# First mixer of a fused network on one core: attention and scan heads taken two at a time

## The chip, the cores and the metric

One core of a Trainium2 chip runs the whole network in one launch. The metric is device time in microseconds (us), from the runs of the program on that core: smaller is better. TensorE (PE in the views) multiplies, VectorE (DVE) and ScalarE (ACT) do the elementwise work, and one queue of transfers (SP) moves data between HBM and the on-chip memory. The products of TensorE land in PSUM, which has eight banks.

## The reference

Two blocks of layers stand behind one another, on 256 tokens of 1024 features, in float32. The first layer's mixer is what the change touches. It projects the normed input and has two branches of 16 heads with 64 features each:

```python
def na_branch(qkv, rpb):           # attention in a window of a 2-D grid
    ...
        s = jnp.einsum('bwhd,biwjhd->bhwij', q_r, k_win) + bias.transpose(0, 2, 1, 3)[None]
        p = jax.nn.softmax(s.reshape(Bsz, NA_HEADS, GRID_W, kh * NA_KW), axis=-1).reshape(s.shape)
        return jnp.einsum('bhwij,biwjhd->bwhd', p, v_win)

def ssd_scan(xh, dt, a, bm, cm):   # state space scan, run in both directions
    ...
    cb = jnp.einsum('bctgn,bcsgn->bgcts', Cc, Bc)
    y_diag = jnp.einsum('bgrcts,bcsgrp->bctgrp', cb[:, :, None] * Lmat, X)
```

The two results are normed, joined and multiplied with an output matrix. The kernel computes the scan of a head as one 256 by 256 matrix of decays (both directions added) times `cb`, applied to the head's 64 columns of tokens; and the attention of a head as full 256 by 256 scores with a bias that is -1e30 outside of the window.

## The kernel before, in words

Weights come in units of 1 MB ([128, 2048] float32). Each unit is split on chip into a high and a low part (`wh` by ACT on line 350, `wl` by DVE on line 359, two halves each), and each large product is three TensorE products of high and low parts. These are the rows `mm<-...` in the views.

`mixer0` (line 960) walks 21 such units in the order of `M0_ORDER` (line 28): four units for the scan's input (`in_x`, line 1105), four gates (`in_z`), and four times q, k, v for four attention heads each (`in_na`, line 1127). Between units, `tick` runs steps of small chains, which are Python generators: `ssd_heads` (line 1026) and `na_heads` (line 1075), one head per step, four heads per chain, so sixteen heads in each branch.

A step of attention (`step` on line 1082) loads the head's bias (`nb`, 256 KB, line 1085, two buffers), multiplies q and k into a PSUM tile `sp` (line 1088, on 64 rows of the array: the head's 64 features lie in partitions 0 to 63 or 64 to 127), adds the bias and takes the row maxima on DVE (line 1091), runs exponentials, division and four transposes of the result (`softmax_T`, line 913; ACT line 350, PE line 369), copies the transposed table to `smp`, and multiplies it with v into half of the partitions of `yp` (line 1096, on 64 columns of the array).

A step of the scan (line 1030) loads the cumulative decays as a broadcast (`bp`, line 1033, two buffers), builds the exponentials (`decay`, line 945), multiplies them with `cb` into `qt`, and multiplies `qt` with the tokens `xt` into half of the partitions of its `yp` (line 1043, on 64 columns).

These small products are in float32, not split: one instruction of the program shows as two rows in the trace, so that a head of each of the three kinds (scores `ax<-nk,nq`, values `ax<-smp,nv`, scan `ax<-qt,xt`) has two instructions and four rows.

The order of the instructions on each engine is fixed when the program is built, by a scheduler that may move instructions past one another where their data permit; `issue_after` and `order` (line 884) bind it. On the chip each engine takes its instructions in that order. Four PSUM banks (`mm`) are for large products, four (`ax`) for everything else. `conv_tile` (line 933) uses padded buffers `cvp` (line 993), three in rotation.

Of the kernel before, what the change touches and what calls it, by code (L numbers as in the profile page):

```python
# [26 lines left out]
# order of the steps of the first mixer (x, z, q/k/v of attention; b: further background) and of the third one  # L27
# [3 lines left out]
# heads of the memory's keys and values that are projected at the ends of the layers' parts  # L31
FILLERS = [("k0 k1", "mm"), ("v0 v1", "ax"), ("k2 k3", "mm"), ("v2 v3", "ax")]
# units of the gated feed-forward that are computed by tokens first, and how many of them wait for their transposes
# [12 lines left out]
# ---------------------------------------------------------------- layout of the inputs  # L46
# [33 lines left out]
# the projections of the third mixer: name, first column, number of columns  # L80
# [11 lines left out]
def _units(w):  # L92
    """[1024, 256 m] -> m units [128, 8 * 256]"""
    m = w.shape[1] // T
    return w.reshape(8, P, m, T).transpose(2, 1, 0, 3).reshape(m, P, 2048)


def _down(w):
    """[256 m, 1024] -> m units [128, 2 * 1024]"""
    m = w.shape[0] // T  # L100
    return w.reshape(m, 2, P, D).transpose(0, 2, 1, 3).reshape(m, P, 2048)


def _square(w):
    """[512, 512 m] -> m units [128, 4 * 512]"""
    m = w.shape[1] // 512
    return w.reshape(4, P, m, 512).transpose(2, 1, 0, 3).reshape(m, P, 2048)
# [13 lines left out]
def prepare(i):  # L121
# [114 lines left out]
    # neighbourhood bias: entry (row distance, column distance), NEG outside of the window  # L236
# [29 lines left out]
# ---------------------------------------------------------------- the program  # L266

class Stack:
# [31 lines left out]
    # ---- small helpers  # L300
# [5 lines left out]
    def phase(self, name, mm=4, apart=(), swap=False):  # L306
        """tiles that live within one phase of the program; mm of the eight banks are for the large products;
        apart: tags with pools of their own, so that they lie where the neighbouring phases leave room in time"""
# [65 lines left out]
    # ---- steps of a chain that are put between the units of the large products  # L374
# [3 lines left out]
    def tick(self, n=1, background=1):  # L378
        """n steps of the chains in order (a chain that yields True waits for others), some of the background's
        (fractions add up)"""  # L380
# [21 lines left out]
    @contextmanager  # L402
    def held(self, on=True):
        """what is traced here is issued after the norm that ended the last phase"""
        with ExitStack() as st:
            for ins in self.hold if on else ():
                st.enter_context(self.tc.issue_after(ins.ins))
            yield

    def lagged(self, steps):  # L410
        """generator: each step's second part after the next one's first part"""
# [17 lines left out]
    # ---- weights: a unit is [128, 2048], taken as high and low parts in two halves  # L429
# [24 lines left out]
    def small_unit(self, name):  # L454
        """generator: a few columns for all inputs, in pieces of 512 of a tile's columns"""
# [11 lines left out]
    def proj_tok(self, u, xh, xl, kind="mm", after=False):  # L467
        """256 columns of x @ W -> [128 tokens, 2, 256]; after: behind the last phase's products, returns also
        the last product"""
# [12 lines left out]
    def proj_feat(self, u, xh, xl):  # L482
        """256 columns of x @ W -> [128 features, 2, 256 tokens]"""
# [11 lines left out]
    def proj_blocks(self, units, rows):  # L495
        """generator: as proj_feat for some units and proj_rows for one small one (rows: name, PSUM), two blocks of 128
        inputs at a time; the sums of one bank are one group, opened by the first product"""
# [24 lines left out]
    def proj_half(self, u, yh, yl):  # L522
        """512 columns of y [512 features] @ W -> two tiles [128 features, 2, 256 tokens]"""
# [14 lines left out]
    def down(self, units, acc, first, last):  # L538
        """acc[t][c] += y @ W with 256 rows of W each (units: (u, yh, yl), y [128, 2, 256]), one half
        of the tokens after the other"""  # L540
# [15 lines left out]
    def out_units(self, name, ys, order, tick=0, tail=2, early=0):  # L556
        """accumulators of y @ W; ys[j] is filled by the chains"""
# [23 lines left out]
    # ---- 1/sqrt(v*inv + eps) to float32 accuracy: a first guess from the exponent, then a  # L581
    # polynomial in v*guess^2 (its leading coefficient folded into the scale of v)
# [19 lines left out]
    # ---- split of a float32 value into two float32r parts (src may be in PSUM)  # L602
# [4 lines left out]
    def first_norm(self):  # L607
        """generator: rms norm of x, transposed, and the modulation of the first mixer (shift and scale), two
        blocks of 128 features at a time; scaled and shifted -> self.xh, self.xl"""
# [54 lines left out]
    def rms(self, x, xn):  # L664
        """1 / root mean square of the rows of x (xn: room for the squares)"""
# [39 lines left out]
    # ---- modulation: sums over the 1024 inputs of silu(c) * ada_w  # L705
# [9 lines left out]
    def cond_first(self, out):  # L715
        """silu(c) along the row on every partition, kept in DRAM"""
# [7 lines left out]
    def cond_row(self, out):  # L724
        """silu(c) along the row, on every partition"""
        self.nc.sync.dma_start(out=out, in_=self.crow_d[0].partition_broadcast(P))
        self.crow = out

    def ada(self, layer, chunks, G=None, kind="ax"):
        """generator: a[.], b[.] columns of both norms and the rows of both gates"""  # L730
# [43 lines left out]
    # ---- x += G * rmsnorm(acc), or x += acc; then the norm of the next block  # L774
# [25 lines left out]
    # ---- layer 1 and 2: feed-forward  # L800
# [27 lines left out]
    # ---- softplus(v) and log_sigmoid(v)  # L828
# [12 lines left out]
    # ---- keys and values of the memory  # L841
    def mem_norm(self):
        """the normalised memory (features on partitions), kept in DRAM"""
# [17 lines left out]
    def mem_fill(self, what, kind, mh, ml):  # L861
        """keys (k) or values (v) of some heads, kept in DRAM, right behind the last phase's products; the first
        transposes of its norm come behind the first head's products, the others anywhere"""
# [20 lines left out]
    def order(self, later, first):  # L884
        """later is issued behind first on their engine"""
        self.tc.add_manual_dep(later.ins, first.ins.name, NOSYNC, reason="issue order")

    def qk_norm(self, ps, out, g, nh, kind="mm"):
        """per-head rms norm of 256 columns (nh heads), transposed, times the gain -> out [128, 2, 256]"""
# [23 lines left out]
    def softmax_T(self, s, src, nm, sign, tp, on_act=False):  # L913
        """softmax of sign*src [128, 2, 256] over the last axis (nm: minus the row maxima), by way of s,
        transposed through the bank tp -> [128 keys, 2, 256 queries]"""
# [16 lines left out]
    # ---- first mixer: state space scan in both directions and neighbourhood attention  # L932
    def conv_tile(self, ps, pre, ft, out):
        """depthwise convolution of width 5 over tokens, bias, silu (channels on partitions)"""
# [10 lines left out]
    def decay(self, A, bp, cc, h):  # L945
        """exponentials of bp (by destination) + cc (by source) in both directions, blocks of 128:
        forward (0,0) (0,1), backward (1,0) (1,1), backward (0,0), forward (1,1) as (source, destination)"""
# [12 lines left out]
    def mixer0(self, tick, nb, late):  # L960
# [4 lines left out]
        # time steps  # L965
# [27 lines left out]
        pre = [self.pt(f"cvp{i}", [P, T + 4]) for i in range(3)]  # L993
# [3 lines left out]
        # B and C  # L997
# [28 lines left out]
        def ssd_heads(c):  # L1026
            """4 heads"""
            yp = self.ax((P, 2, T))

            def step(hh):  # L1030
# [8 lines left out]
                self.tt(M.rearrange("p s t -> p (s t)"), A[:, 0:512], cb[c // 2].rearrange("p s t -> p (s t)"), ALU.mult)  # L1039

                b = 64 * (hh % 2)
                for s in range(2):
                    self.matmul(yp[b:b + 64, hh // 2], xt[c][:, s, hh * 64:(hh + 1) * 64], M[:, s], s == 0, s == 1)
                if hh % 2:
                    f = hh // 2
# [7 lines left out]
        def ssd_finish():  # L1053
            # the sum of squares of 2 y silu(z) over the channels, on every partition
# [20 lines left out]
        def na_heads(c, q, k, v):  # L1075
# [6 lines left out]
            def step(hh):  # L1082
                h, b, f = c * 4 + hh, 64 * (hh % 2), hh // 2
                bias = self.pt("nb", [P, 2, T], bufs=2)
                nc.sync.dma_start(out=bias, in_=self.a["nab"][h].rearrange("p (t k) -> p t k", t=2))
                sp = self.ax((P, 2, T))
                for t in range(2):
                    self.matmul(sp[:, t], q[b:b + 64, f, t * P:(t + 1) * P], k[b:b + 64, f])
                nm = self.sm(2, "nam")
                for t in range(2):  # L1090
                    nc.vector.tensor_tensor_reduce(out=bias[:, t], in0=sp[:, t], in1=bias[:, t], scale=-1.0, scalar=3.0e38,
                                                   op0=ALU.add, op1=ALU.min, accum_out=nm[:, t:t + 1])

                pt = self.softmax_T(bias, bias, nm, -1.0, sp, True)
                for kt in range(2):
                    self.matmul(yp[b:b + 64, f], v[:, kt, hh * 64:(hh + 1) * 64], pt[:, kt], kt == 0, kt == 1)
                if hh == 3:
                    self.split(yh, yl, yp)
                    ys[4 + c] = (yh, yl)

            for hh in range(4):
                step(hh)
                yield

        def in_x(c):
# [3 lines left out]
            for f in range(2):  # L1109
                self.conv_tile(ps[:, f], pre[(2 * c + f) % 3], 4 + 2 * c + f, xc[:, f])  # L1110
# [39 lines left out]
    # ---- second mixer: mLSTM in both directions  # L1150
    def mixer1(self, tick, nb):
# [4 lines left out]
        # gates: rows 0-7 forward, 32-39 backward  # L1156
# [747 lines left out]
```

## Time and profile before

| what | value |
|---|---|
| time, median of 3 runs | 1548.85 us (1548.67 to 1549.3) |
| span of the profiled execution, first to last instruction | 1547.9 us |
| PE busy over the span | 1488.8 us |
| DVE busy over the span | 1166.1 us |
| ACT busy over the span | 855.9 us |
| granted TensorE clock, mean | 0.996 |

The page gives no other time of the profiled execution than its span. A busy engine is one with an instruction in flight; PE's products are pipelined and overlap, so its pace is read from the distance between the starts of rows, and not from their lengths. In the rows of a timeline the columns are the start, the length, the engine, the line, the operation, the tile written and the tiles read, the shape and the number of instructions merged into the row; a bracket tells how long the engine was idle before and what released it.

### The profile page before, as it was taken

To read this page: it belongs to the slowest core of one execution; us is meant where nothing else is said; L and a number is where in the kernel's file an instruction comes from. 1 tells how busy PE (TensorE), PEld (TensorE's weight loads), DVE (VectorE), ACT (ScalarE), POOL (GpSimd) and SP (SyncE) were. 2 spreads that over 40 slices of the span, in tenths; PEclk is the share of its full clock that TensorE was granted. 3 is DMA by queue.
4 is the path that set the end of the run, shared out by engine and by line. 5 is a ranking of instruction groups with operands and counts; after the bars stand their busy time and mean duration, and the time that the engine had idled before them with its cause. 6 is when DMAs were issued, how large, how long until landed. Compare 5 with 4: busy or idle time off the path is not lost.

```text
span 1547.9 us, 25416 instructions
## 1 busy us (share of the span) xinstructions
PE 1488.8 (96%) x9964; PEld 1325.5 (86%) x9964; DVE 1166.1 (75%) x2223; ACT 855.9 (55%) x1502; POOL 4.5 (0%) x26
## 2 busy tenths in 40 slices
PE   2899999999999989999999999999999999999999
PEld 2878887898898889998889989877789999799998
DVE  8788878877778896667988866858888987565555
ACT  4776765654546555554756765445444456454443
POOL 0000000000000000000000000000000000000000
PEclk9999999999999999999999999989999999999999
DMA  9656777577886785446576665323343355235552
GB/s 351 236 136 190 267 280 265 199 300 275 327 298 224 269 296 190 142 160 204 221 268 230 236 227 191 126 93 112 127 157 109 134 208 204 109 137 191 184 178 101
DMA packets 62058, 315.47 MB, mean 204 GB/s; under 512 B 6385, under 2 KB 15217, under 8 KB 28146
## 3 DMA queue, kind: packets, MB, share of 16 engines
q1 hardware_dynamic: 61938, 313.85, 57.5%
q8 instruction: 78, 1.28, 0.3%
q14 instruction: 42, 0.34, 0.1%
HBM read 304.77 MB, written 9.05 MB: 203 GB/s over the span
## 4 chain that ended last, share of the span: by engine, by line
PE 80%; DVE 11%; DMA 4%; ACT 3%; issue 2%; SPq 0%; ACTq 0%; DVEq 0%
PE mm L365 51%; PE ax L365 26%; DVE wl L359 2%; PE ax L369 2%; DMA bp<-cs_d 1%; DMA raw<-in_ada 1%; DVE acc L750 1%; ACT xn L350 1%; ACT wh L350 1%; DVE acc L637 1%; DMA bp<-nM_d 1%; DVE cva L362 0%; DVE qt L359 0%; DMA nb<-in_nab 0%; PE mm L369 0%
## 5 line engine op out<-in xcount | busy, mean ns | idle before, releaser
L359 DVE TENSOR_TENSOR wl<-raw,wh 128x1024 fp32r<-128x1024 f32 x400 | 485.5, 1222 | 202.2 <-ACT wh L350 201.6
L350 ACT ACTIVATE wh<-raw 128x1024 fp32r<-128x1024 f32 x400 | 419.5, 1057 | 369.3 <-PE mm L365 208.5
L365 PE MATMUL mm<-xh,wh 128*128 128x256 f32 x1536 | 441.3, 287 | 3.8 <-ACT bp L350 2.8
L365 PE MATMUL mm<-xh,wl 128*128 128x256 f32 x1536 | 439.3, 286 | 0.5 <-DVE wl L359 0.4
L365 PE MATMUL mm<-xl,wh 128*128 128x256 f32 x1536 | 439.4, 286 | 0.0
L365 PEld LDWEIGHTS mm<-xh,wh 128*128 128x128 f32 x1536 | 296.5, 193 | 13.8 <-issue 6.8
L365 PEld LDWEIGHTS mm<-xl,wh 128*128 128x128 f32 x1536 | 296.6, 193 | 7.8 <-issue 6.0
L365 PEld LDWEIGHTS mm<-xh,wl 128*128 128x128 f32 x1536 | 296.4, 193 | 5.3 <-issue 3.6
L365 PE MATMUL mm<-wh,xh 128*128 128x256 f32 x496 | 143.3, 289 | 0.0
L365 PE MATMUL mm<-wl,xh 128*128 128x256 f32 x496 | 141.8, 286 | 0.3 <-DVE wl L359 0.2
L365 PE MATMUL mm<-wh,xl 128*128 128x256 f32 x496 | 141.2, 285 | 0.0
L365 PE MATMUL ax<-wh,mhh 128*128 128x512 f32 x256 | 102.4, 400 | 0.0
L365 PE MATMUL ax<-wl,mhh 128*128 128x512 f32 x256 | 101.3, 396 | 0.0
L365 PE MATMUL ax<-wh,mhl 128*128 128x512 f32 x256 | 101.3, 396 | 0.0
L365 PEld LDWEIGHTS mm<-wl,xh 128*128 128x128 f32 x496 | 94.9, 191 | 3.4 <-issue 2.3
L365 PEld LDWEIGHTS mm<-wh,xh 128*128 128x128 f32 x496 | 94.8, 191 | 3.0 <-issue 2.5
L365 PEld LDWEIGHTS mm<-wh,xl 128*128 128x128 f32 x496 | 94.9, 191 | 1.6 <-issue 1.5
L365 PEld LDWEIGHTS ax<-wh,mhl 128*128 128x128 f32 x256 | 48.1, 188 | 12.0 <-DVE mhl L359 0.4
L365 PEld LDWEIGHTS ax<-wh,mhh 128*128 128x128 f32 x256 | 48.2, 188 | 10.7 <-ACT wh L350 0.5
L365 PEld LDWEIGHTS ax<-wl,mhh 128*128 128x128 f32 x256 | 48.1, 188 | 10.7 <-issue 0.5
L362 DVE SCALAR_TENSOR_TENSOR acc<-raw,cond,acc 128x1024 f32<-128x1024 f32 x28 | 35.8, 1278 | 9.3 <-DMA raw<-in_ada 9.1
L750 DVE CUSTOM_DVE_ANT_0 acc<-raw,crow 128x1024 f32<-128x1024 f32 x32 | 39.0, 1219 | 2.4 <-DMA raw<-in_ada 2.1
(486 smaller groups left out, 2601.4 us busy)
## 6 DMA issues: line engine op xcount, KB each, us to landing
raw<-in_wts SPq DMA_DIRECT2D x214, 1024.0 KB, 4.9
raw<-in_ada SPq DMA_DIRECT2D x48, 1024.0 KB, 6.0
nb<-in_nab SPq DMA_DIRECT2D x16, 256.0 KB, 2.9
grow<-in_rows SPq DMA_DIRECT2D x16, 256.0 KB, 5.1
bp<-cs_d SPq DMA_DIRECT2D x16, 256.0 KB, 6.2
s5tab<-s5t SPq DMA_DIRECT2D x16, 256.0 KB, 2.5
s5tl<-s5tab SPq DMA_DIRECT2D x16, 256.0 KB, 2.9
meml<-mem_d SPq DMA_DIRECT2D x2, 1024.0 KB, 6.2
```

The source lines that it names most:

```text
L350: return self.nc.scalar.activation(out=out, in_=in_, func=func, **kw)
L359: return self.nc.vector.tensor_tensor(out=out, in0=in0, in1=in1, op=op)
L362: return self.nc.vector.scalar_tensor_tensor(out=out, in0=in0, scalar=s, in1=in1, op0=op0, op1=op1)
L365: return self.nc.tensor.matmul(out, lhsT, rhs, start=start, stop=stop)
L369: return self.nc.tensor.transpose(out, in_, self.ident[0:k, 0:k])
L637: nc.vector.tensor_tensor_reduce(out=acc, in0=raw[:, k * D:(k + 1) * D], in1=self.crow, scale=1.0, scalar=0.0, op0=ALU.mult, op1=ALU.add, ...
L750: nc.vector.tensor_tensor_reduce(out=acc, in0=w, in1=self.crow, scale=1.0, scalar=0.0, op0=ALU.mult, op1=ALU.add, accum_out=s8[:, j:j + 1])
```

## The change

The two chains work on two heads at a time. For attention, the biases of both heads are loaded and both scores are multiplied first, the instructions of the upper half of the array (partitions 64 to 127) and of the lower half in turn; then comes the softmax of one head, a step's end, the softmax of the other, and the value products of both, again in turn. For the scan the products of two heads are issued in turn once both have their table. A new helper `after` ties the order of the four instructions of a pair. There are four buffers of `nb` in place of two, and two of `cvp` in place of three. All else in the diff is comments taken out.

```diff
+NB_BUFS = 4
...
+    def after(self, first, later):
+
+        if first is None:
+            return later
+        self.order(later, first)
+        return first
...
-        pre = [self.pt(f"cvp{i}", [P, T + 4]) for i in range(3)]
+        pre = [self.pt(f"cvp{i}", [P, T + 4]) for i in range(2)]
...
             yp = self.ax((P, 2, T))
+            Ms = []
...
-                b = 64 * (hh % 2)
-                for s in range(2):
-                    self.matmul(yp[b:b + 64, hh // 2], xt[c][:, s, hh * 64:(hh + 1) * 64], M[:, s], s == 0, s == 1)
+                Ms.append(M)
                 if hh % 2:
-                    f = hh // 2
+
+                    f, first = hh // 2, None
+                    for s in range(2):
+                        for i in (1, 0):
+                            b, g = 64 * i, 2 * f + i
+                            first = self.after(first, self.matmul(yp[b:b + 64, f], xt[c][:, s, g * 64:(g + 1) * 64], Ms[i][:, s],
+                                                                  s == 0, s == 1))
+                    Ms.clear()
...
-            def step(hh):
-                h, b, f = c * 4 + hh, 64 * (hh % 2), hh // 2
-                bias = self.pt("nb", [P, 2, T], bufs=2)
-                nc.sync.dma_start(out=bias, in_=self.a["nab"][h].rearrange("p (t k) -> p t k", t=2))
-                sp = self.ax((P, 2, T))
+            def pair(f):
+
+                bias, sp, pts, first = [], [], [], None
+                for i in range(2):
+                    bias.append(self.pt("nb", [P, 2, T], bufs=NB_BUFS))
+                    nc.sync.dma_start(out=bias[i], in_=self.a["nab"][c * 4 + 2 * f + i].rearrange("p (t k) -> p t k", t=2))
+                    sp.append(self.ax((P, 2, T)))
                 for t in range(2):
-                    self.matmul(sp[:, t], q[b:b + 64, f, t * P:(t + 1) * P], k[b:b + 64, f])
-                nm = self.sm(2, "nam")
...
+                    for i in (1, 0):
+                        b = 64 * i
+                        first = self.after(first, self.matmul(sp[i][:, t], q[b:b + 64, f, t * P:(t + 1) * P], k[b:b + 64, f]))
+                for i in range(2):
+                    nm = self.sm(2, "nam")
...
+                    pts.append(self.softmax_T(bias[i], bias[i], nm, -1.0, sp[i], True))
+                    if i == 0:
+                        yield
+                first = None
                 for kt in range(2):
-                    self.matmul(yp[b:b + 64, f], v[:, kt, hh * 64:(hh + 1) * 64], pt[:, kt], kt == 0, kt == 1)
-                if hh == 3:
+                    for i in (1, 0):
+                        b, hh = 64 * i, 2 * f + i
+                        first = self.after(first, self.matmul(yp[b:b + 64, f], v[:, kt, hh * 64:(hh + 1) * 64], pts[i][:, kt], kt == 0, kt == 1))
+                if f == 1:
...
-                self.conv_tile(ps[:, f], pre[(2 * c + f) % 3], 4 + 2 * c + f, xc[:, f])
+                self.conv_tile(ps[:, f], pre[f], 4 + 2 * c + f, xc[:, f])
```

The scheduler sets a new order. It differs from the old one in the first mixer and at its end, up to the start of the feed-forward behind it; what follows has the same order as before. The number behind a tile's name tells one tile from another; the line numbers of the changed kernel are larger by one and more.

On TensorE, second group of four attention heads (`nv_1379` before, `nv_1374` now): before, the values of its first head, then the scores of the three others, one head after the other (`ax_1546` on the lower half, `ax_1631` on the upper, and so on).

```order
L369 MATMUL ax_1523<-cst_80,nb_1521 128x128 x2
...
L365 MATMUL mm_1816<-xh_108,wh_1819 128x256
L365 MATMUL ax_1520<-smp_1540,nv_1379 64x256 x2
L365 MATMUL ax_1546<-nk_1284,nq_1190 128x256 x2
L365 MATMUL ax_1631<-nk_1284,nq_1190 128x256 x2
L365 MATMUL ax_1654<-nk_1284,nq_1190 128x256 x2
L365 MATMUL mm_1816<-xl_109,wh_1819 128x256
```

The same place now:

```order
L366 MATMUL ax_1517<-smp_1558,nv_1374 64x256
L366 MATMUL ax_1517<-smp_1542,nv_1374 64x256
...
L366 MATMUL ax_1631<-nk_1279,nq_1185 128x256
L366 MATMUL ax_1628<-nk_1279,nq_1185 128x256
...
L366 MATMUL ax_1737<-qt_1764,xt_1489 64x256
L366 MATMUL ax_1737<-qt_1750,xt_1489 64x256
```

The first pair's values, the second pair's scores and a pair of the scan stand next to one another, each as four instructions that alternate between the halves (each two rows come twice). All 24 pairs of the mixer have this form, but in two pairs of scores transposes of the scan stand between the instructions, as here, in the first pair of the same group:

```order
L370 MATMUL ax_1490<-cst_80,xs_1468 128x128
L366 MATMUL ax_1523<-nk_1279,nq_1185 128x256
L370 MATMUL ax_1490<-cst_80,xs_1468 128x128 x3
L366 MATMUL ax_1520<-nk_1279,nq_1185 128x256
L366 MATMUL ax_1523<-nk_1279,nq_1185 128x256
L366 MATMUL ax_1520<-nk_1279,nq_1185 128x256
L366 MATMUL mm_1676<-xl_109,wh_1679 128x256
```

On the queue of transfers, the stretch in which the biases `nb` of the second pair of heads (before) are loaded, among decays `bp` and weights `raw`:

```order
L437 DMA raw_1226<-in_wts 128x2048
L1085 DMA nb_825<-in_nab 128x512
L1033 DMA bp_1115<-cs_d_433 128x2x256
L1033 DMA bp_1192<-cs_d_433 128x2x256
L1085 DMA nb_848<-in_nab 128x512
L1033 DMA bp_1209<-cs_d_433 128x2x256
L437 DMA raw_1321<-in_wts 128x2048
L1085 DMA nb_1521<-in_nab 128x512
```

Now, at the same place:

```order
L1042 DMA bp_1112<-cs_d_433 128x2x256
L438 DMA raw_1221<-in_wts 128x2048
L1100 DMA nb_1518<-in_nab 128x512
L1100 DMA nb_1521<-in_nab 128x512
L1042 DMA bp_1187<-cs_d_433 128x2x256
L438 DMA raw_1316<-in_wts 128x2048
L1042 DMA bp_1206<-cs_d_433 128x2x256
L438 DMA raw_1410<-in_wts 128x2048
```

The biases of the first four heads (`nb_825` and `nb_848` among them before) have been loaded at the start of the mixer, in place of the first two; those loaded here belong to the second group. Each bias is issued one pair of heads earlier than before.

## Rows read from the trace of the kernel before

**Rows 1.** The page, busy time by engine

```profile
PE 1488.8 (96%) x9964; PEld 1325.5 (86%) x9964; DVE 1166.1 (75%) x2223; ACT 855.9 (55%) x1502; POOL 4.5 (0%) x26
```

**Rows 2.** Busy us per stretch: PE, weight loads, DVE, ACT, POOL, clock, DMA share, GB/s

```profile
50.00:250.00 200.00, 188.93 (x1309) 159.86 (x1308) 165.60 (x374) 140.17 (x311) 0.00 (x0) 1.00 0.67 222
...
126.00:151.40 25.40, 25.20 (x174) 21.21 (x174) 22.88 (x46) 16.28 (x34) 0.00 (x0) 1.00 0.63 208
...
163.90:190.50 26.60, 26.60 (x185) 21.67 (x185) 23.48 (x57) 17.54 (x44) 0.00 (x0) 1.00 0.79 281
...
203.30:228.50 25.20, 25.20 (x180) 21.71 (x181) 17.18 (x36) 16.80 (x34) 0.00 (x0) 1.00 0.75 274
```

**Rows 3.** PE's small products, 57 to 270 us, grouped by shape

```profile
L365 PE MATMUL ax<-smp,nv 128*64 128x256 f32 x64 | 17.2, 392 | 2.5 <-ACT smp L350 2.5
...
L365 PE MATMUL ax<-qt,xt 128*64 128x256 f32 x64 | 15.8, 393 | 1.5 <-DVE qt L359 1.5
L365 PE MATMUL ax<-nk,nq 64*128 64x256 f32 x64 | 12.8, 397 | 0.0
```

**Rows 4.** PE's timeline, a scan head alone between large products

```profile
116.67 0.28 PE L365 MATMUL mm<-xh,wl 128*128 128x256 f32 x1
116.80 0.28 PE L365 MATMUL mm<-xh,wh 128*128 128x256 f32 x1
117.00 1.08 PE L365 MATMUL ax<-qt,xt 128*64 128x256 f32 x4
118.01 0.39 PE L365 MATMUL mm<-xl,wh 128*128 128x256 f32 x1
```

**Rows 5.** PE's timeline, two scan heads next to one another

```profile
108.68 0.28 PE L365 MATMUL mm<-xl,wh 128*128 128x256 f32 x1
108.89 1.09 PE L365 MATMUL ax<-qt,xt 128*64 128x256 f32 x8
109.91 0.39 PE L365 MATMUL mm<-xh,wl 128*128 128x256 f32 x1
```

**Rows 6.** PE's timeline, the scores of one head

```profile
218.40 1.13 PE L365 MATMUL ax<-nk,nq 64*128 64x256 f32 x4
219.46 0.39 PE L365 MATMUL mm<-xh,wh 128*128 128x256 f32 x1
```

**Rows 7.** PE's timeline, the scores of three heads

```profile
158.55 1.99 PE L365 MATMUL ax<-nk,nq 64*128 64x256 f32 x12
160.47 0.39 PE L365 MATMUL mm<-xl,wh 128*128 128x256 f32 x1
```

**Rows 8.** PE's timeline, the values of one head

```profile
209.55 1.08 PE L365 MATMUL ax<-smp,nv 128*64 128x256 f32 x4
210.56 0.39 PE L365 MATMUL mm<-xl,wh 128*128 128x256 f32 x1
```

**Rows 9.** PE's timeline, two of its waits in the mixer

```profile
126.02 1.08 PE L365 MATMUL ax<-qt,xt 128*64 128x256 f32 x4 [1.52 <-DVE qt L359]
...
163.85 0.44 PE L369 MATMUL ax<-cst,nb 128*128 128x128 f32 x2 [1.22 <-ACT nb L350]
```

**Rows 10.** The chain that ended last, 40 to 330 us: start, us, what

```profile
116.73 6.68 DMA bp<-cs_d
...
156.38 5.82 DMA nb<-in_nab
```

**Rows 11.** Waits of the transfer queue, 30 to 300 us: total, times, longest

```profile
SPq L1085 <- PE ax L369: 40.7, 12, 6.7
```

**Rows 12.** ACT, 57 to 270 us, the softmax and the weight split

```profile
L350 ACT ACTIVATE wh<-raw 128x1024 fp32r<-128x1024 f32 x48 | 50.0, 1052 | 18.1 <-PE mm L365 14.1 <-issue 3.8
L350 ACT ACTIVATE nb<-nb,nam 128x256 f32<-128x256 f32 x32 | 15.9, 500 | 6.7 <-DVE nam L1091 6.7
L350 ACT ACTIVATE nb<-nb,smr 128x256 f32<-128x256 f32 x32 | 14.4, 500 | 2.6 <-DVE smr L920 2.6
...
L350 ACT ACTIVATE smp<-ax 128x512 f32<-128x512 f32 x16 | 9.5, 591 | 5.4 <-PE ax L369 5.3
```

More of the change, by code (lines that the diff above doesn't have):

```diff
@@ L1080, in na_heads @@
             yp = self.ax((P, 2, T))
-            def step(hh):
-                h, b, f = c * 4 + hh, 64 * (hh % 2), hh // 2
-                bias = self.pt("nb", [P, 2, T], bufs=2)
-                nc.sync.dma_start(out=bias, in_=self.a["nab"][h].rearrange("p (t k) -> p t k", t=2))
-                sp = self.ax((P, 2, T))
-                for t in range(2):
-                    self.matmul(sp[:, t], q[b:b + 64, f, t * P:(t + 1) * P], k[b:b + 64, f])
-                nm = self.sm(2, "nam")
[L1090 to L1094, printed above, removed]
+            def pair(f):
[4 more added lines that the diff above has]
+                    sp.append(self.ax((P, 2, T)))
+                for t in range(2):
+                    for i in (1, 0):
[3 more added lines that the diff above has]
+                    nm = self.sm(2, "nam")
+                    for t in range(2):
+                        nc.vector.tensor_tensor_reduce(out=bias[i][:, t], in0=sp[i][:, t], in1=bias[i][:, t], scale=-1.0, scalar=3.0e38,
+                                                       op0=ALU.add, op1=ALU.min, accum_out=nm[:, t:t + 1])
+                    pts.append(self.softmax_T(bias[i], bias[i], nm, -1.0, sp[i], True))
+                    if i == 0:
+                        yield
+                first = None
@@ L1095, in step @@
                 for kt in range(2):
-                    self.matmul(yp[b:b + 64, f], v[:, kt, hh * 64:(hh + 1) * 64], pt[:, kt], kt == 0, kt == 1)
-                if hh == 3:
+                    for i in (1, 0):
+                        b, hh = 64 * i, 2 * f + i
+                        first = self.after(first, self.matmul(yp[b:b + 64, f], v[:, kt, hh * 64:(hh + 1) * 64], pts[i][:, kt], kt == 0, kt == 1))
+                if f == 1:
                     self.split(yh, yl, yp)
                     ys[4 + c] = (yh, yl)
-            for hh in range(4):
-                step(hh)
@@ L1103, in na_heads @@
                 yield
+            for f in range(2):
+                yield from pair(f)
         def in_x(c):
```

## The prediction, made before the changed kernel ran

> **What bounds the kernel now.** I read the page first: PE is busy 96% of the span, DVE 75%, ACT 55% [rows 1]. PE sets the pace nearly everywhere, so time taken off PE is time off the kernel, unless another engine is close behind in that very place. So the second view is the busy time by stretch in the first mixer. From 50 to 250 us PE is busy 188.93 of 200 us, DVE 165.60 and ACT 140.17, at the full granted clock of 1.00, the 2.4 GHz level [rows 2]. DVE is at 83% there, more than its 75% over the span. In three stretches that PE fills without a wait it has 22.88 of 25.40 us, 23.48 of 26.60 and 17.18 of 25.20 [rows 2]: 90%, 88% and 68%. The reader should see that PE leads, and that in places its lead over DVE is a tenth.
>
> Third, what the small products cost. Each kind has 64 rows, 16 heads of four [rows 3]. Large products start 0.13 us apart (116.67 to 116.80), and a scan head that stands alone has its first start at 117.00 and the next large product at 118.01 [rows 4]: 1.01 us, and 0.20 ahead of it in place of 0.13. Two scan heads next to one another take from 108.89 to 109.91 [rows 5]: 1.02 us for eight rows. The two heads lie on different halves of the array's columns, and the second is free. A head of values takes 1.01 us, 209.55 to 210.56 [rows 8]; a head of scores 1.06, 218.40 to 219.46 [rows 6]; three heads of scores 1.92, 158.55 to 160.47 [rows 7], which is 1.26 us less than three times 1.06, so two of them share the array as well, on different halves of its rows. The order before has those heads one behind the other, not in turn; that they are neighbours is enough.
>
> Fourth, PE's waits in the mixer. They are short: 1.52 us for a table of the scan, 1.22 us for a softmax [rows 9]. Near the first the chain of waits holds a transfer of decays of 6.68 us, ahead of the second a bias of 5.82 us [rows 10].
>
> **The change, part by part.**
>
> *Small products.* A head alone takes 0.20 + 1.01 = 1.21 us from the large product ahead to the one behind [rows 4]; without it these would be 0.13 apart, so it costs 1.08 us (1.13 for scores, by 1.06 in place of 1.01). A pair costs 0.21 + 1.02 - 0.13 = 1.10 us [rows 5]; for a pair of scores I take 1.14, a head alone plus 0.01; three heads of scores cost 1.92 + 0.07 = 1.99. I counted along PE's timeline; of each pattern one stands in [rows 4 to 8]. Scores: five heads alone, one pair, three times three heads. Values: 15 alone, one that shares the array with a scan head. Scan: 11 alone, one pair, the one with that head of values, and two cut up by transposes, for which I take 1.7 us, between a pair's 1.10 and two alone, 2.16. Before: scores 5 x 1.13 + 1.14 + 3 x 1.99 = 12.8; values and scan 26 x 1.08 + 2 x 1.10 + 1.7 = 32.0. After: 8 x 1.14 + 16 x 1.10 = 26.7. PE saves 18.1 us. In two pairs of scores transposes stand between the instructions; each pair is left and entered once more, by [rows 4] about 0.2 + 0.2 us, so 0.8 us comes off: 17.3 us. That instructions alternate I cost at nothing: the rows of neighbours already start together.
>
> The Trainium skill (TensorE: Matmul & The Clock Gate, part 3, what overlaps and what doesn't) has a rule against this: weight loads overlap running products only where the row group differs, and two halves of the columns share their rows. The trace does not agree, with eight rows in 1.02 us [rows 5]. By the rule the 16 pairs of values and scan would save nothing, and the sum would keep the scores' 12.8 - 9.1 = 3.7 us at most.
>
> *What of it reaches the end.* Where PE waits for a chain that began long before, its saving only lengthens the wait. Of some 36 heads that stand alone, 24 lie in stretches where the chain of waits runs through PE itself (83 to 94, 126 to 151, 164 to 190 and 203 to 254 us); as 12 pairs they save 12 x (2.16 - 1.10) = 12.7 us. The other 4.6 us lie ahead of waits such as those of [rows 9], and I count none of it.
>
> Then DVE. From 126 to 151 us six heads would save 3.2 us, and 25.40 would be 22.2, but DVE has 22.88 us to do; from 164 to 190 it is 26.60 - 3.2 = 23.4 against 23.48 [rows 2]. Nor can DVE be busy all the time, since it takes turns with ACT and PE on the same tiles: I take off 1.5 us in each, 3.0 in all. From 203 to 228 DVE has room.
>
> *Biases.* The queue waited 12 times, 40.7 us in total, to load a bias until PE's transposes had read the old one, with weights and decays queued behind it [rows 11]. With four buffers it waits for the pair before, which is done earlier. PE's wait of 1.22 us [rows 9] that follows a bias of 5.82 us [rows 10] should go: 1.2 us gained. Two more biases, 0.5 MB, go ahead of a weight unit at the start of the mixer, while two rows of gates, 0.5 MB, move behind that unit: even.
>
> *Softmax.* The values of a pair wait for both softmaxes. A head costs ACT two exponentials and two scalings of 0.50 us and a copy of 0.59 [rows 12], 2.6 us, and in the new order the first head's scalings mostly stand behind both heads' exponentials. The scheduler put more large products between scores and values (53 in place of 37 in the first pair, though 19 up to the first transpose in the seventh). I charge 0.1 us a pair, 0.8 us; the bounds are nothing, where the products cover it, and 2.6 us a pair.
>
> *Scan.* A product of two heads comes between 20 large products before and 44 behind the place where the second head's stood; the sum on DVE that reads both heads waited for the second anyway. Nothing; what covers it is that nobody else reads `yp`.
>
> *Padded buffers.* ACT may fill one when DVE has read it two convolutions earlier, which is one unit back: 96 large products, 12 us at 0.13 [rows 4]. Nothing, as long as units are that far apart.
>
> *Sum.* 12.7 - 3.0 + 1.2 - 0.8 = 10.1 us off the span of 1547.9 us, which is 0.95 us under the median of the runs: 1548.85 - 10.1 = 1538.75; I say 1538.5. Less than 0.2%, 3.1 us, is what a measurement here could not tell from no change.
>
> **The rivals.**
>
> *All of it arrives.* The waits of [rows 9] hang on transfers whose issue stands behind work that PE releases, so they move up too. For it: the weight split waited 14.1 us in total for PE's products [rows 12], so weights were early. Against it: DVE's share. Gain 15 us to 17.3 plus the 2.7 us of [rows 9]: 1529 to 1534.
>
> *DVE and the transfers take PE's place.* DVE's 166 us in a stretch that would be 200 - 17 = 183 long are 91%, and the transfer of decays keeps its two buffers and its 6.68 us [rows 10]. Then the stretches end when DVE ends, and 3 to 7 us are left: 1542 to 1546. For it: the 90% of [rows 2]; against it: the 68%.
>
> *The second softmax comes onto PE's path.* PE takes its instructions in order, so a pair's values that find no second `smp` hold all large products behind them. The price is up to 2.6 us for each of eight pairs, 20.8 us. From 2.2 us a pair on, 17.3 / 8, the gain is used up; at the full price, with DVE's 3.0 us, it is 1548.85 + 20.8 + 3.0 - 17.3 = 1555. For it: PE has already waited for a softmax [rows 9], and in the tightest place only 27 large products, 3.5 us, stand between a pair's scores and values. Against it: in most places some 50 do, 6.5 us.
>
> *Only half of the mechanism works.* If two heads on different column halves hindered each other, other than in [rows 5], which is one place, only the scores would gain: 3.7 us, of which half arrives: 1547. This is what the rule above would give.
>
> **How the numbers follow.** The forecast, 8 to 14 us gained, gets 0.56; all arrives 0.15; DVE and transfers 0.19; the second softmax 0.07; half of the mechanism 0.03. The range, 1530.5 to 1546, takes in the first two rivals but for an outer end, and leaves out the last two. The forecast's own range is 1535 to 1541. Faster is 0.56 + 0.15 + 0.19 less 0.06 for small gains at the weak end: 0.84; slower 0.07; within 0.2% the 0.06 and the last rival's 0.03: 0.09.
>
> **What would show it.** Right: in PE's timeline groups of eight rows of each small kind, with the next product 1.0 to 1.1 us after the first start; the mixer ends 8 to 14 us earlier and the rest is as long as before; DVE is 88 to 93% busy from 126 us on; the queue's waits for transposes fall well below 40.7 us. Wrong: groups of eight that take 2 us; waits of PE for `smp` or `nb` of over 2 us in most pairs; or waits for `wl` of several us, which would make DVE the bound.

## The result and the profile after

| | kernel before | changed kernel |
|---|---|---|
| median of the runs, us | 1549.07 (1548.67 to 1549.82, 4 runs) | 1537.72 (1534.84 to 1539.51, 4 runs) |
| ratio, 95% interval | | 0.9908 [0.9881, 0.9936] |
| a second comparison | 1549.78 (11 runs) | 1540.80 (6 runs), 0.9939 [0.9924, 0.9954] |
| profiled execution: span | 1547.9 | 1533.0 (own time 1534.84) |

The medians differ by 11.35 us and, in the second comparison, by 8.98 us. The ratios, which are estimated from the single runs, stand for 14.3 and 9.5 us, 0.9 and 0.6%. Single runs of one kernel lie several us apart, and a part of that is TensorE's clock, which falls to its 1.2 GHz level in other places in each execution: the profiled execution before has a granted clock of 0.50 from 1017.3 to 1027.6 us, that after has 1.00 there (last of the stretches below). From the end of the first mixer on, where the order differs only at the start, the execution before takes 1242.0 us (1547.9 less 305.93) and that after 1238.0 (1533.0 less 295.00), so 4.0 of the 14.9 us between the two spans lie outside of the mixer. In the 14 profiled executions of this document that part takes 1236 to 1248 us; the four with less than 1239 us (the changed kernel, e8_again, e3_att, e7_nb3) are the four that keep the full clock between 1000 and 1040 us.

The place to compare is therefore the end of the first mixer. In the chain that ended last, the first long piece of large products behind it and the transposes that follow (start us, us, what), of the kernel before:

```profile
305.93 11.29 PE mm L365 x92
317.21 0.44 PE mm L369 x4
```

and of the changed kernel, with two transfers that lie on its chain earlier:

```profile
115.02 4.77 DMA bp<-cs_d
...
122.07 6.93 DMA bp<-cs_d
...
295.00 11.70 PE mm L366 x94
306.70 0.44 PE mm L370 x4
```

The mixer ends 10.9 us earlier by the starts of the two pieces, which do not begin with the same product, and 10.5 by the transposes. The changed kernel's page by engine, which answers to [rows 1]; PE is 15.9 us less busy, DVE as long as before:

```profile
PE 1472.9 (96%) x9964; PEld 1318.1 (86%) x9964; DVE 1164.9 (76%) x2223; ACT 854.5 (56%) x1502; POOL 4.5 (0%) x24
```

PE's small products, 57 to 260 us, grouped by shape, to be set beside [rows 3]:

```profile
L366 PE MATMUL ax<-nk,nq 64*128 64x256 f32 x64 | 10.5, 406 | 0.0
L366 PE MATMUL ax<-qt,xt 128*64 128x256 f32 x64 | 9.6, 424 | 4.1 <-DVE qt L360 4.1
L366 PE MATMUL ax<-smp,nv 128*64 128x256 f32 x64 | 8.7, 392 | 0.0
```

They were busy for 17.2 + 15.8 + 12.8 = 45.8 us and are now for 28.8: 17.0 us less. PE's timeline shows how a pair looks, and the large product behind it: first scores, then values, then the one scan pair that waits:

```profile
74.26 1.13 PE L366 MATMUL ax<-nk,nq 64*128 64x256 f32 x8
75.32 0.39 PE L366 MATMUL mm<-xh,wh 128*128 128x256 f32 x1
...
83.39 1.08 PE L366 MATMUL ax<-smp,nv 128*64 128x256 f32 x8
84.40 0.39 PE L366 MATMUL mm<-xh,wl 128*128 128x256 f32 x1
...
118.28 0.28 PE L366 MATMUL mm<-wh,xh 128*128 128x256 f32 x1
122.66 1.97 PE L366 MATMUL ax<-qt,xt 128*64 128x256 f32 x8 [4.09 <-DVE qt L360]
124.56 0.58 PE L366 MATMUL mm<-wl,xh 128*128 128x256 f32 x1
```

Eight rows and 1.06 or 1.01 us to the next product, as a single head took before [rows 4, 6, 8]. The last three rows are the new thing: PE stands for 4.09 us before a scan pair, and the pair behind that takes 1.90 us in place of 1.01. The stretches say why (columns as in [rows 2]); behind the wait the granted clock is 0.50, the 1.2 GHz level:

```profile
50.00:250.00 200.00, 187.48 (x1351) 163.43 (x1350) 176.08 (x396) 144.67 (x318) 0.00 (x0) 0.97 0.69 232
...
121.65:128.48 6.83, 5.82 (x26) 4.69 (x27) 4.56 (x11) 1.53 (x4) 0.00 (x0) 0.50 0.41 125
...
126.00:151.40 25.40, 24.00 (x175) 21.19 (x175) 22.86 (x55) 16.81 (x39) 0.00 (x0) 0.95 0.60 209
151.40:190.00 38.60, 37.29 (x296) 32.72 (x295) 36.72 (x97) 29.70 (x78) 0.00 (x0) 1.00 0.87 290
...
1017.30:1027.60 10.30, 10.30 (x57) 7.05 (x56) 4.81 (x15) 5.32 (x14) 0.00 (x0) 1.00 0.22 89
```

From 50 to 250 us DVE now has 176.1 us of work in place of 165.6, and PE 187.5 in place of 188.9. What PE waits for, 57 to 270 us (total, times, longest), first in the kernel before:

```profile
PE ax L369 <- ACT nb L350: 2.5, 2, 1.3
PE ax L365 <- ACT smp L350: 2.5, 1, 2.5
PE ax L365 <- DVE bc L362: 2.1, 1, 2.1
PE ax L365 <- DVE qt L359: 1.5, 1, 1.5
PE mm L365 <- DVE wl L359: 0.9, 3, 0.4
```

and in the changed kernel:

```profile
PE ax L366 <- DVE qt L360: 4.1, 1, 4.1
PE mm L366 <- DVE wl L360: 2.7, 4, 0.8
PE ax L370 <- ACT nb L351: 1.7, 3, 1.1
PE mm L366 <- ACT wh L351: 0.7, 1, 0.7
PE ax L366 <- DVE bc L363: 0.7, 1, 0.7
```

The sum hardly moves (9.5 us before, 10.2 after, with one row of 0.3 that isn't shown), but its kind does: waits for the softmax (`smp`, and `nb`, the bias's tile, which holds its exponentials when PE transposes them) gave way to waits for a table and for weights' low parts, both made by DVE. The wait for `bc`, B and C of the scan, is short here and 2.3 us in the second profiled execution (e8_again). The transfer queue's longest waits, 30 to 300 us, first one row of the kernel before, to be set beside [rows 11]:

```profile
SPq L437 <- DVE wl L359: 42.1, 16, 5.1
```

and in the changed kernel:

```profile
SPq L438 <- DVE wl L360: 64.5, 15, 16.5
...
SPq L1100 <- PE ax L370: 18.0, 7, 4.7
```

It waits 22.7 us less to load biases, until PE's transposes have read the old ones, and 22.4 us more to load weights, until DVE has made the low parts of the old ones.

### The profile page after: what moved, and what is told of

Same layout as the page of the kernel before. It is cut to its first block, busy times and chain, and to the rows that moved or that the text cites. A ratio compares the mean times of both kernels' runs of the same rounds, so it can differ in the third digit from the quotient of the medians.

```text
span 1533.0 us, 25395 instructions
## 1 busy us (share of the span) xinstructions
PE 1472.9 (96%) x9964; PEld 1318.1 (86%) x9964; DVE 1164.9 (76%) x2223; ACT 854.5 (56%) x1502; POOL 4.5 (0%) x24
## 4 chain that ended last, share of the span: by engine, by line
PE 77%; DVE 12%; DMA 5%; ACT 5%; issue 2%; SPq 0%; ACTq 0%; DVEq 0%
PE mm L366 50%; PE ax L366 24%; DVE wl L360 3%; PE ax L370 2%; DMA bp<-cs_d 1%; ACT xn L351 1%; ACT wh L351 1%; DMA raw<-in_ada 1%; DVE acc L751 1%; ACT nb L351 1%; DMA grow<-in_rows 1%; DVE acc L638 1%; DMA raw<-in_wts 1%; DMA bp<-nM_d 1%; PE mm L370 0%
```

## The experiments

All times stand beside runs of the kernel before on the same chip, whose median is in the third column. Four groups were measured apart (e1 to e4; e5 to e8; e9 and e10; e11 and e12), so across groups the ratios are compared; a saving in us in the text below is the ratio's. The last column is the start of the first long piece of large products behind the mixer, in one profiled execution each (305.93 before, 295.00 after; 296.09 when the changed kernel was profiled again).

| kernel | median us | kernel before | ratio, 95% interval | mixer's end |
|---|---|---|---|---|
| e1_bufs | 1547.10 | 1548.81 | 0.9984 [0.9969, 0.9999] | 303.49 |
| e2_noshare | 1550.76 | 1548.81 | 1.0001 [0.9982, 1.0021] | 310.85 |
| e3_att | 1543.07 | 1548.81 | 0.9969 [0.9952, 0.9987] | 296.57 |
| e4_scan | 1553.65 | 1548.81 | 1.0036 [1.0023, 1.0050] | 307.70 |
| e8_again | 1540.80 | 1549.78 | 0.9939 [0.9924, 0.9954] | 296.09 |
| e5_held | 1539.17 | 1549.78 | 0.9928 [0.9907, 0.9949] | 296.36 |
| e6_bp3nb3 | 1536.52 | 1549.78 | 0.9913 [0.9894, 0.9931] | 295.07 |
| e7_nb3 | 1539.17 | 1549.78 | 0.9922 [0.9902, 0.9942] | 295.29 |
| e9_late | 1544.45 | 1548.82 | 0.9963 [0.9944, 0.9982] | 298.81 |
| e10_late_bp3 | 1538.83 | 1548.82 | 0.9918 [0.9895, 0.9940] | 292.69 |
| e11_lessdve | 1534.55 | 1550.89 | 0.9889 [0.9876, 0.9901] | 292.53 |
| e12_before_lessdve | 1550.56 | 1550.89 | 0.9998 [0.9985, 1.0011] | 308.45 |

The theory behind all of them: the time comes from two heads sharing the array. The first four ask whether it is that, or the buffers and the order that came with it.

**The buffers alone.**

```diff
-                bias = self.pt("nb", [P, 2, T], bufs=2)
+                bias = self.pt("nb", [P, 2, T], bufs=4)
-                self.conv_tile(ps[:, f], pre[(2 * c + f) % 3], 4 + 2 * c + f, xc[:, f])
+                self.conv_tile(ps[:, f], pre[f], 4 + 2 * c + f, xc[:, f])
```

> The kernel before with the buffers of the change alone: four bias tiles and two padded convolution tiles; every head is still handled by itself. Theory (the time comes from two heads' products sharing the array): 0 to 2 us under the kernel before, 1547 to 1549 us, since only PE's waits for a late bias can go; the 8-row groups stay as before. Rival (the earlier bias loads and the shorter queue give the time): at least half of the 11.35 us, 1543.5 us or less.

0.9984, which is 2.5 us and hardly surer than nothing. The rival falls: the buffers are not where most of the time comes from.

**No sharing.**

```diff
-                        b = 64 * i
+                        b = 64
...
-                for kt in range(2):
-                    for i in (1, 0):
-                        b, hh = 64 * i, 2 * f + i
-                        first = self.after(first, self.matmul(yp[b:b + 64, f], v[:, kt, hh * 64:(hh + 1) * 64], pts[i][:, kt], kt == 0, kt == 1))
+                for i in (1, 0):
+                    for kt in range(2):
+                        n = 64 * (i + 1)
+                        first = self.after(first, self.matmul(yp[0:n, f], v[:, kt, 128 * f:128 * f + n], pts[i][:, kt], kt == 0, kt == 1))
```

(and the scan's products like the values')

> The changed kernel, with its buffers, its order of two heads at a time and as many small products, but a pair's products cannot share the array: scores of both heads use the upper half of the rows (so the scores of one head of each pair are computed twice and those of the other not at all; the work is the same), and in scan and values one head's product uses all 128 columns, the other one's 64. Theory (sharing): the gain is gone, 24 pairs x 1.08 us of PE come back, less what hides in PE's waits: 1546 to 1554 us; a pair takes 2.0 to 2.1 us from its first start to the next product in place of 1.01 to 1.06. Rival (order and buffers give the time): it stays at 1538 to 1541 us.

1.0001: the whole gain is gone. PE's timeline of this kernel, a pair of scores and a pair of values:

```profile
75.85 1.99 PE L366 MATMUL ax<-nk,nq 64*128 64x256 f32 x8
77.77 0.39 PE L366 MATMUL mm<-xh,wh 128*128 128x256 f32 x1
...
85.11 2.03 PE L366 MATMUL ax<-smp,nv 128*128 128x256 f32 x8
87.07 0.39 PE L366 MATMUL mm<-xh,wl 128*128 128x256 f32 x1
```

1.92 and 1.96 us where the changed kernel takes 1.06 and 1.01. The buffers, the number of products and the order of the pairs in the program are the same, only the halves are taken away; the scheduler set the pairs at somewhat other places among the large products. So sharing is the cause, shown.

**Attention alone, scan alone.** The diff is the change's own hunk for `na_heads`, or that for `ssd_heads`, without the other.

> Attention on two heads at a time with four bias tiles and two padded tiles, the scan as before one head at a time. Theory: scores save 3.7 us of PE and values 16 x 1.08 - 8 x 1.10 = 8.5 us; with the share that arrived in the whole change (11 of 17 us) 6 to 9 us under the kernel before, 1540 to 1543 us; and the wait of 4.09 us on the scan's second table is not there, so it may be as fast as the whole change. Rival (the scan's pairs carry half of it or more): no more than 5.5 us, 1543.5 us or above.

> The scan on two heads at a time, attention as before one head at a time with two bias tiles; two padded tiles. Theory: the scan's pairs save about 6 us of PE, and the wait for the second head's table (4.09 us in the changed kernel, with half clock behind it) takes most of it back: 0 to 3 us under the kernel before, 1546 to 1549 us, and a wait of 3 us or more on a table of the scan stands near 120 us. Rival (the scan's pairs arrive as the forecast counted them, at no charge): 4 to 6 us, 1543 to 1545 us, and no such wait.

Attention alone, with its four bias tiles, gives 0.9969, 4.8 us (5.7 by the medians). Its interval, 2.0 to 7.4 us, takes in a part of both expectations, so it doesn't show that the scan's pairs carry half. Its profiled execution, the fastest of the twelve with 1534.59 us, speaks against half: there the mixer ends at 296.57 us, 9.4 us earlier than before and 0.5 to 1.6 us later than in the changed kernel. How the gain divides stays open. Scan alone is 5.6 us slower, which neither expected, and the wait I had charged it with isn't there. PE's waits of that kernel, 57 to 310 us, and its scan products:

```profile
PE mm L366 <- DVE wl L360: 5.0, 5, 1.6
...
PE mm L366 <- ACT wh L351: 1.8, 2, 1.4
```

```profile
L366 PE MATMUL ax<-qt,xt 128*64 128x256 f32 x64 | 10.2, 412 | 0.0
```

The scan's products fell from 15.8 to 10.2 us, and PE waited instead for weights (5.0 us for low parts, 0.9 before). Its mixer ends 1.8 us later than before. Behind the mixer, where nothing was changed, its profiled execution takes 1247.7 us in place of 1242.0: it has 13.7 us at half clock there in place of 10.2, which is 1.7 us, and I can't explain the rest. What follows: the two halves of the change do not add up (4.8 less 5.6 is not 9 to 14). That the saving is worth what the next chain lets through is my reading of it, not shown by it.

**Is it the turn or the neighbourhood?** With the changed kernel once more beside it.

```diff
-                for t in range(2):
-                    for i in (1, 0):
+                for i in (1, 0):
+                    for t in range(2):
```

(the loops of values and scan likewise)

> The changed kernel with each pair still held together, but one head's two instructions behind the other head's two, not in turn. Theory (being neighbours on different halves suffices, the forecast's claim): a pair still takes 1.01 to 1.07 us from its first start to the next product, and the time is within 2 us of the changed kernel, apart from waits that the scheduler's other order makes. Rival (alternating is what lets them share): a pair takes 1.5 to 2.1 us, and at least half of the gain, 5 us or more, is lost.

> The changed kernel itself once more, beside the three kernels below. Theory: 9 to 12 us under the kernel before, as in its first comparison, and in its profile the same wait of about 4 us for a scan pair's second table near 120 us. Rival (half of the first difference was a matter of where TensorE's granted clock fell in those few runs): 5 to 8 us.

The changed kernel repeats: 0.9939, 9.5 us, with a wait of 4.30 us at the same place. Without the turns the time is the same, 0.9928, and a pair of values takes 1.02 us:

```profile
83.19 1.09 PE L366 MATMUL ax<-smp,nv 128*64 128x256 f32 x8
84.21 0.39 PE L366 MATMUL mm<-xh,wl 128*128 128x256 f32 x1
```

Being neighbours on different halves is enough. (One of the 24 pairs, of scores, came apart in this kernel's order.)

**The wait for the scan's table.** First theory: the decays' transfers. `bp` gets a third tile; one bias tile goes to make room, hence the control.

```diff
-NB_BUFS = 4
+NB_BUFS = 3
...
-                bp = self.pt("bp", [P, 2, T], bufs=2)
+                bp = self.pt("bp", [P, 2, T], bufs=3)
```

> The changed kernel with three tiles for the scan's decays in place of two, and three bias tiles in place of four, so that it fits. Theory (the wait of 4.09 us on the second table is the transfer of decays, which waits for one of its two tiles): the wait falls under 1.5 us, TensorE's granted clock stays at 1.00 behind it, and the kernel is 3 to 7 us faster than the one below with three bias tiles alone. Rival (with the decays there early, the transfers' bandwidth or VectorE is late in the same place): a wait of 3 us or more stays near 120 us, and the two kernels are within 2 us.

> The changed kernel with three bias tiles in place of four, the control for the kernel above. Theory (the gain is the shared array, and a third tile already takes the load out of the queue's way): within 2 us of the changed kernel. Rival (both biases of the next pair have to be there early): each of the seven later pairs starts behind the transpose of the pair before, the waits for a late bias come back, and it is 3 us or more slower than the changed kernel.

Three bias tiles do as well as four. With the third decay tile the chain before the pair no longer holds a transfer (start us, us, what):

```profile
119.75 0.69 DVE qt L360
120.44 1.58 DVE xn L363 x6
122.02 0.35 DVE xn L360
...
122.63 0.61 DVE qt L360
123.28 1.98 PE ax L366 x8
```

but PE still waits (57 to 270 us):

```profile
PE ax L366 <- DVE qt L360: 3.0, 1, 3.0
PE mm L366 <- DVE wl L360: 2.7, 5, 0.8
```

3.0 in place of 4.1 us, and the clock falls behind it all the same (columns as in [rows 2]):

```profile
122.70:129.53 6.83, 6.25 (x28) 5.11 (x29) 5.89 (x15) 2.91 (x8) 0.00 (x0) 0.50 0.63 166
```

1536.52 stands against the control's 1539.17 us, with overlapping intervals. The wait is the rival's; the 2.65 us lie between its 2 and the theory's 3. DVE makes both tables in the last 4 us before the pair; the transfer had only been the last of several things to come.

Second theory: the pair stands too early in PE's order.

```diff
+            for hh in range(4):
+                step(hh)
+                if hh == 2:
+                    pair(0)
+                yield
+            pair(1)
```

> The changed kernel with a scan pair's products written one step later: behind the table of the next head for the first pair, behind the chain's last step for the second; four bias tiles and two decay tiles as in the change. Between the second pair's place near 120 us and its tables there are then some 45 large products in place of some 10. Theory (the wait of 4 us is a matter of place: the products stand in TensorE's order ahead of tables that VectorE and the decays deliver later, and nobody needs them so early): the wait falls under 1 us, the granted clock stays at 1.00 there, and it is 4 to 7 us faster than the changed kernel, 1532 to 1536 us. Rival (the tables are late because VectorE is full, and whatever follows waits for it instead): waits of the same 3 to 5 us in total stand at weights' low parts between 115 and 160 us, and the time is within 2 us of the changed kernel.

> The same later place for a scan pair's products, together with three decay tiles and three bias tiles. Theory (place): as fast as the kernel above within 2 us, since the decays then have time anyway. Rival (the decays' transfers are the cause that matters): 3 us or more faster than the kernel above.

It fell too. The later place isn't faster than the change but slower, 0.9963 (its interval lies apart from that of the first comparison of the change and overlaps that of the second), and PE's waits, 57 to 270 us, are longer:

```profile
PE mm L366 <- DVE wl L360: 6.3, 4, 4.2
PE ax L366 <- DVE qt L360: 3.1, 1, 3.1
```

With the third decay tile beside it the table's wait is gone, and the same time is lost to the weights' low parts:

```profile
PE mm L366 <- DVE wl L360: 6.5, 6, 2.7
```

It is 5.6 us faster than e9_late by the medians, with intervals apart, which is what the rival expected: at the later place the decays' transfers count. But at 0.9918 it is no better than the change, although in its profiled execution the mixer ends at 292.69 us, 2.3 to 3.4 us earlier. Served earlier or moved, the wait comes back at another thing that DVE makes; that speaks for DVE itself as a bound.

**Less work for DVE, in both kernels.** The theory left.

```diff
-                ends = A[:, 0:512].rearrange("p (i n) -> p i n", n=P)[:, 0:4:3]
-                self.tt(ends, ends, A[:, 512:768].rearrange("p (i n) -> p i n", n=P), ALU.add)
```

> The changed kernel without VectorE's addition of the second part of the scan's diagonal blocks (128x256, 16 of 0.42 us, 6.7 us of VectorE between 84 and 175 us); the scan's tables leave that part out. Theory (behind the saved PE time VectorE's chains are the next bound in the first mixer, which is why 17.3 us saved gave some 10): the mixer ends 3 to 7 us earlier than in the changed kernel, 1532 to 1537 us. Rival (PE still bounds it, or the transfers do): within 2 us of the changed kernel.

> The kernel before without the same addition, 6.7 us of VectorE less. Theory (there PE bounds the mixer, VectorE only in short places): 0 to 2.5 us under the kernel before, 1546.5 to 1549 us, clearly less than the same cut brings in the changed kernel. Rival (VectorE was as much a bound before the change): 3 us or more.

The same cut, 6.7 us of DVE, brings nothing in the kernel before (0.9998) and something in the changed one: 0.9889 against 0.9908 and 0.9939, with a mixer that ends at 292.53 in place of 295.00 and 296.09 us, 2.5 to 3.6 us earlier, where the theory had 3 to 7. In the kernel before with the cut, PE stays full where DVE had room made (columns as in [rows 2]):

```profile
126.00:151.40 25.40, 25.40 (x179) 21.65 (x179) 21.42 (x48) 17.22 (x38) 0.00 (x0) 1.00 0.64 207
```

DVE's 22.88 us [rows 2] became 21.42 and PE's 25.20 became 25.40. So before the change PE bounded this stretch. That behind the change DVE is a part of the bound is likely, and not shown, for four reasons. The scheduler makes another order when instructions go, and in the kernel before that moved the mixer's end by as much the other way: 308.45 in place of 305.93. e10_late_bp3, which takes nothing off DVE, ends its mixer at 292.69, as early as e11_lessdve. The addition stands in the chain that makes a scan's table, so without it this chain is shorter, and not only DVE less busy. And the interval of e11_lessdve overlaps that of the first comparison of the change, not that of the second.

None of the kernels that compute everything is surely faster than the change; e6_bp3nb3 has the lowest median of them, 1536.52, inside the others' intervals.

## Why the prediction was right, and where not

The forecast was 10.1 us, to 1538.5; by the medians 11.35 and, in the second comparison, 8.98 us were measured. Its steps:

- *PE saves 17.3 us.* Right: 17.0 by the rows, in which one pair at half clock costs 0.9. The pairs take 1.01 and 1.06 us as read from [rows 5, 7], and e2_noshare shows that without the sharing nothing of the time is left.
- *Alternating costs and gives nothing.* Right, by e5_held.
- *The column halves overlap.* Right. The Trainium skill (TensorE: Matmul & The Clock Gate, part 3, what overlaps and what doesn't) lets weight loads overlap running products only on different row groups. The trace does not agree: 15 of the 16 pairs on column halves take 1.01 us, at the full clock, and such pairs 1.96 once the halves are taken away; the weight loads of the first scan pair run from 104.55 to 105.18 us, while its products run. That by the rule these pairs would save nothing was my own conclusion.
- *12.7 us of it arrive, 4.6 lie ahead of waits.* Too careful, as far as the rows tell. PE's wait of 2.5 us for a softmax's `smp` is gone in both executions of the changed kernel, and that for `nb` is 1.7 and 1.9 us in place of 2.5: some of what lay ahead of waits arrived too. That these waits hung on work that PE released is argued; how much of the 4.6 us came in isn't measured.
- *Scan: nothing.* This step failed. I looked at who reads the pair's result, not at what the pair needs: PE takes its instructions in order, so a product that waits for two tables holds every large product behind it. It cost 4.09 us of waiting against 1.5 before, and then the clock: 5.82 of the 6.83 us at half speed lie behind the wait, which are 2.9 us of work lost. Together that is up to 5.5 us that the sum did not have.
- *DVE takes off 3.0 us.* Likely right in kind, though e11_lessdve and e12_before_lessdve do not show it. Not in place: from 126 to 151 us DVE has the same 22.86 us, 90%, and from 151 to 190 us 36.72 of 38.60, 95%, but PE loses the time at single tables and low parts rather than evenly.
- *Biases, 1.2 us.* 0.8 us by PE's rows for `nb`; with the whole queue's relief 2.5 us in e1_bufs, from almost nothing to 4.8. The waits of the queue for transposes fell from 40.7 to 18.0 us, as said; those for DVE's low parts rose by as much.
- *Softmax, 0.8 us.* Nothing: no row of values waits for `smp` in the changed kernel.
- *Padded buffers, nothing.* Not tried by themselves; e1_bufs has them and is not slower.

So two errors met: some of the 4.6 us that I left out came in, and up to 5.5 us that I took for nothing went out. The main mechanism was right; that the sum came out so near is partly luck. From 17.0 us of rows, with 2.0 off for the half clock behind the wait outside the pair and 0.7 for the longer waits, 14.3 are left, and the mixer ended 10.5 to 10.9 earlier. Of the other 3.4 to 3.8 us up to 1.7 may be a second stretch at half clock, from 56.8 to 60.2 us, which neither the kernel before nor e8_again has; I can't place the rest. The rival "DVE and the transfers take PE's place" names what PE then waited for, but its price was too high.

## What to carry to other kernels

Two products that use different halves of the array's rows or columns cost here as much as one when they are neighbours in TensorE's order (1.01 and 1.06 us for a pair as for a head); look for half-empty arrays, and count a saving of about one head for each pair. When two products are joined, the pair waits for the later one's operand with everything behind it: price each joined group by its last input. And when the leading engine is relieved by a tenth, test the next one by taking a known piece of work off it in both kernels, and hold the order of the rest fixed while you do: here the scheduler's new order moved the mixer's end by as much as the cut, so the test did not decide. A single profiled execution of each kernel can't decide it either.

## What the runs showed of the hardware

A wait of PE costs more than its length when the clock falls behind it, and not always by as much. Stretches behind the wait for the scan's table, in the first execution of the changed kernel (wait 4.09 us):

```profile
122.60:128.50 5.90, 5.84 (x26) 4.71 (x27) 3.61 (x9) 1.00 (x3) 0.00 (x0) 0.50 0.41 133
```

and in its second (wait 4.30 us):

```profile
122.60:128.50 5.90, 4.82 (x27) 3.68 (x28) 4.63 (x11) 1.53 (x4) 0.00 (x0) 0.71 0.51 117
```

The same wait was followed by half clock throughout in one and for a part in the other. The Trainium skill (TensorE: Matmul & The Clock Gate, part 1, HAM oscillation) says that waits between bursts of products put the clock back to half; these rows agree. The kernel before, whose waits in the mixer were at most 2.5 us, ran its stretches at 1.00 [rows 2]. The length of one wait alone does not tell: behind a wait of 2.46 us for `smp` at 83.30 us the kernel before stayed at 1.00, and behind one of 2.46 us for `bc` at 70.23 us e6_bp3nb3 had 0.50 from 71.5 to 74.9 us.
